# First layer's output projection in blocks of seven products, with ten low parts of weights by a negated copy and a transfer

## The chip, the cores and the metric

The kernel runs on one core of a Trainium2 chip. The metric is device time in microseconds (us) from start to end of one launch. The kernel before took 1089.74 us, the median of three runs (1089.67 to 1090.6). The core has five engines that run side by side, each through its own queue and in order: TensorE (PE in the profile) multiplies matrices and writes only to PSUM, VectorE (DVE) and ScalarE (ACT) do elementwise work, GpSimd (POOL) mostly issues transfers here, and SyncE (SP) issues the loads. An engine waits for another through a semaphore.

## The reference

Two transformer layers on 512 tokens of width 1024, in float32. Only the first layer's mixing matters here:

```python
proj = a @ w_in_a[layer]
u, v, q_mem = proj[..., :768], proj[..., 768:1536], proj[..., 1536:]
main = chunked_spatial_gating(u, v, w_s, b_s, ln_g, ln_b)     # 768 features: six groups of 128
mixed = concatenate([main, memory_attention(q_mem, mem_n, w_mem_kv[layer])], axis=-1)
h = h + rmsnorm(mixed @ w_out[layer], ln_mix_post[layer])     # the output projection: 1024 x 1024
```

After it comes a feed-forward (gate, up, down, with 2816 hidden features), then a second layer with causal attention in place of the gating.

## The kernel before, in words

**Precision.** TensorE is used in a reduced float32 type, so each operand `x` is kept as two parts: `hi`, a cast by ScalarE, and `lo = x - hi`, a subtraction by VectorE. The helper `split` makes both (L239), and `mm3` (L191 to L193) makes one product of three matmuls: hi by hi, hi by lo and lo by hi. Nearly all of the program's arithmetic runs through these two helpers, so the lines L191, L192, L193 and L239 stand for many places, and the tiles' names tell which: `whi`/`wlo` are parts of weights, `mixedhi`/`mixedlo` of the projection's inputs.

**The projection.** `mixed` is held as eight feature tiles of 128 features by 512 tokens. Tiles 6 and 7 are the memory attention's, 0 to 5 the spatial gating's, and `ORDER` puts 6, 7, 0, 1 first. One output tile `y` is 128 tokens (one of four token blocks, `tb`) by 512 of the 1024 output features (one of two halves, `dh`). In each matmul a 128 x 128 part of a feature tile is the stationary operand and 512 columns of weights are the moving one. `out_part` makes the first half of the sum, over the feature tiles 6, 7, 0, 1: two halves, four token blocks, four feature tiles and three matmuls each, 96 in all. Each finished tile is copied from PSUM to the tile `ys[tb][dh]` (L915). `mix_tail` and `tail_of` later add the feature tiles 2 to 5 (L846) and go on with the norm.

**Where it stands.** At the end of `layer_a` the gate blocks 1 to 5 (`gate_inputs`, 24 matmuls each) are put between the spatial blocks 0 to 5 (`spatial`, eight short matmuls each, then a chain over ScalarE and VectorE to the tile `sgu`, L765 to L770, which `store` splits into a feature tile of `mixed`). The first three spatial blocks lie between gate blocks, the last three between pieces of `out_part`: five, five and six pieces of six matmuls. The memory attention lies ahead of all this; its two feature tiles are put together from pairs of heads by `join` (L423, L424).

**Buffers.** Weights are loaded by SP's queue into four buffers `raw` of 128 x 1024, and their parts lie in eight buffers for `hi` and eight for `lo`, each 128 x 512. Three of these sixteen hold the spatial weights, one for every two spatial blocks: two among the `hi`, one among the `lo`. The activations' parts share 36 buffers, the float tiles `prob` six. PSUM has eight banks under three names: `tr` (2), `mm` (3) and `lg` (3). A buffer is given again when its last reader is done.

**What sets the order.** The program is written once, and a planner of the language lays out each engine's queue from it: at each step an engine gets, of what the planner expects to be ready, what was written first. Blocks under `high_priority` go ahead, and blocks under `issue_after` go behind a named instruction. On the chip the queues are then fixed, so an instruction whose input is late holds up all that stands behind it on its engine. SP's and GpSimd's transfers stand in such queues too.

**A pattern that is there already.** The feed-forward's down projection (`DownSeven`, `down_sevens`) makes 2 x 2 blocks with seven products instead of eight, and its class `Inner` makes some low parts through `split_aside`: ScalarE casts, ScalarE writes the negated high part (L1155), and a GpSimd transfer adds the source onto it in memory (L1156), so that VectorE is not needed. Copies from one PSUM tile to another are at L1270.

Of the kernel before, what the change touches and what calls it, by code (L numbers as in the profile page):

```python
# [7 lines left out]
F32 = mybir.dt.float32  # L8
# [32 lines left out]
def hybrid(ctx: ExitStack, tc: tile.TileContext, i: dict, out: bass.AP):  # L41
# [104 lines left out]

    def prepared(src, shape, aside=False):
# [16 lines left out]
    def moving_pair(src, aside=False):  # L164

        raw = wp.tile([P, 1024], F32, tag="raw", name=name("raw"), bufs=4)
        last_load[0] = nc.sync.dma_start(raw.rearrange("p (m c) -> p m c", m=4), src)
        four = raw.rearrange("p (m k c) -> p m k c", m=4, k=2)
# [69 lines left out]
    def split(src, hi, lo, eng=None):  # L238
        last_parts[:] = A.copy(hi, src), (eng or V).tensor_sub(lo, src, hi)  # L239

# [170 lines left out]

    joined = {}

    def join(o, mixed, m, j):


        own, _ = rows(j)
        if j == 0:
            mixed[m] = act("mixedhi"), act("mixedlo")
# [4 lines left out]
        V.tensor_add(joined[m][own, :], o[:64, :], f[:64, :])  # L424
        if j:
            return lambda: split(joined[m], *mixed[m])
# [163 lines left out]
    def layer_a():  # L590
# [55 lines left out]
        with tc.tile_pool(name="sgu", bufs=1) as lp:  # L646
# [60 lines left out]
            mixed = [None] * KT  # L707
            attend(mem_heads(0, q, mixed), between={n: take(fill, c) for n, c in enumerate((4, 4, 4, 4))})
# [46 lines left out]
            def spatial(g):  # L755
# [15 lines left out]
                store(t2, mixed, g)  # L771
# [124 lines left out]
    def out_part(layer, mixed):  # L896
# [22 lines left out]
        return ys, [block(dh) for dh in range(2)]  # L919

# [195 lines left out]
    def feed_forward(layer, phase, xp, meanwhile=None):  # L1116
# [33 lines left out]

        def split_aside(src, hi, lo, aside):
            if not aside:
                return split(src, hi, lo)
            A.copy(hi, src)
            A.activation(lo, hi, AF.Copy, scale=-1.0)  # L1155
            G.dma_start(lo, src, accum_op=ALU.add)  # L1156
# [485 lines left out]
```

## Time and profile before

| | |
|---|---|
| median of three runs | 1089.74 us |
| the profiled execution's own time | 1089.34 us |
| its span, first to last instruction | 1087.6 us |
| TensorE busy | 1079.2 us, 99% |
| VectorE busy | 971.8 us, 89% |
| ScalarE busy | 755.9 us, 69% |
| GpSimd busy | 93.5 us, 9% |
| granted TensorE clock, mean | 0.999 |

All times inside the profile are counted from the span's first instruction. A row of the instruction list gives the start, the duration, the engine, the line of the kernel, the operation, and `output<-inputs`; a bracket at its end tells how long the engine sat idle before it and who released it. A row of groups gives the count behind an x, then busy time and mean duration in ns. Matmuls overlap in the pipeline and their ends are modelled, so a matmul's pace is the distance between two starts, not its duration. Instructions of VectorE and ScalarE overlap by some 0.1 us in the same way. Rows of transfers give the time from issue to landing.

### The profile page before, as it was taken

The page shows a single profiled execution, that of the slowest core. Times are in us where ns is not written, and L with a number is a line of the kernel's source. Part 1 is how long each engine was busy: PE and PEld are TensorE (multiplying, and loading weights), DVE is VectorE, ACT ScalarE, POOL GpSimd, SP SyncE. Part 2 cuts the span into 40 slices and gives each one's busy share as a digit, 9 for nine tenths or more (in the row PEclk, how much of TensorE's full clock was granted, in tenths as well). Part 3 has the DMA queues.
Part 4 walks back from the last instruction along what each step waited for, and adds up shares of the span by engine and source line. Part 5 has one row for each costly group of instructions (what it writes and reads, how often), then busy time and mean ns, then how long its engine had stood idle before and what let it go on. Part 6 is the DMA issues. An engine that isn't in the chain of part 4 may idle for free.

```text
span 1087.6 us, 19810 instructions
## 1 busy us (share of the span) xinstructions
PE 1079.2 (99%) x7266; PEld 982.4 (90%) x7267; DVE 971.8 (89%) x1942; ACT 755.9 (69%) x1588; POOL 93.5 (9%) x120
## 2 busy tenths in 40 slices
PE   9999999999999999999999999999999999999998
PEld 8998889998989898998988998889997989898996
DVE  7879768999999999997968789868999999999986
ACT  7776578667766667577747788868666666757664
POOL 1000000002020202001000000000002010201100
PEclk9999999999999999999999999999999999999999
DMA  7421441338464664746222654531347465564632
GB/s 272 161 83 42 121 130 39 117 97 194 128 156 129 144 182 97 195 145 187 78 78 61 156 135 125 151 117 40 99 116 173 119 154 158 120 193 94 177 97 78
DMA packets 83993, 139.65 MB, mean 128 GB/s; under 512 B 6772, under 2 KB 49800, under 8 KB 83896
## 3 DMA queue, kind: packets, MB, share of 16 engines
q1 hardware_dynamic: 71480, 116.57, 34.9%
q0 software_dynamic: 11712, 21.50, 11.6%
q8 instruction: 57, 0.93, 0.4%
q10 hardware_dynamic: 704, 0.32, 0.1%
q14 instruction: 40, 0.33, 0.1%
HBM read 105.23 MB, written 2.10 MB: 99 GB/s over the span
## 4 chain that ended last, share of the span: by engine, by line
PE 71%; DVE 19%; DMA 4%; issue 3%; ACT 3%; SPq 0%; DVEq 0%; ACTq 0%
DVE wlo L239 6%; PE y L191 5%; PE y L192 5%; PE y L193 5%; PE ps L191 4%; PE ps L193 4%; PE ps L192 4%; DMA raw<-in_w_gate 4%; PE a L191 3%; PE a L192 3%; PE a L193 2%; PE v L191 2%; PE yc L191 2%; PE v L192 2%; PE v L193 2%
## 5 line engine op out<-in xcount | busy, mean ns | idle before, releaser
L239 ACT CAST whi<-raw 128x512 fp32r<-128x512 f32 x444 | 264.0, 620 | 100.7 <-DVE raw L1045 27.4
L239 DVE TENSOR_TENSOR wlo<-raw,whi 128x512 fp32r<-128x512 f32 x444 | 292.5, 687 | 22.1 <-ACT whi L239 21.2
L191 PE MATMUL x<-xshi,whi 128*128 128x256 f32 x320 | 90.0, 281 | 0.0
L193 PE MATMUL x<-xshi,wlo 128*128 128x256 f32 x320 | 90.0, 281 | 0.0
L191 PE MATMUL a<-xshi,whi 128*128 128x256 f32 x320 | 90.0, 281 | 0.0
L192 PE MATMUL x<-xslo,whi 128*128 128x256 f32 x320 | 89.9, 281 | 0.0
L192 PE MATMUL a<-xslo,whi 128*128 128x256 f32 x320 | 89.8, 281 | 0.0
L193 PE MATMUL a<-xshi,wlo 128*128 128x256 f32 x320 | 89.8, 281 | 0.0
L191 PE MATMUL ps<-xshi,whi 128*128 128x256 f32 (+1 forms) x224 | 68.5, 306 | 0.0
L192 PE MATMUL ps<-xslo,whi 128*128 128x256 f32 (+1 forms) x224 | 66.7, 298 | 0.0
L193 PE MATMUL ps<-xshi,wlo 128*128 128x256 f32 (+1 forms) x224 | 66.4, 298 | 0.0
L239 ACT CAST whi<-s 128x512 fp32r<-128x512 f32 x56 | 34.8, 621 | 38.8 <-DVE s L1208 18.6
L192 PEld LDWEIGHTS a<-xslo,whi 128*128 128x128 f32 x320 | 60.3, 189 | 0.4
L191 PEld LDWEIGHTS a<-xshi,whi 128*128 128x128 f32 x320 | 60.3, 188 | 0.4
L193 PEld LDWEIGHTS x<-xshi,wlo 128*128 128x128 f32 x320 | 60.4, 189 | 0.0
L192 PEld LDWEIGHTS x<-xslo,whi 128*128 128x128 f32 x320 | 60.3, 189 | 0.0
L193 PEld LDWEIGHTS a<-xshi,wlo 128*128 128x128 f32 x320 | 60.3, 189 | 0.0
L191 PEld LDWEIGHTS x<-xshi,whi 128*128 128x128 f32 x320 | 60.3, 188 | 0.0
L1243 POOL DMA_DIRECT2D y<-yo x48 | 41.4, 953 | 192.2 <-ACT yo L1242 130.8
L191 PE MATMUL y<-whi,mixedhi 128*128 128x512 f32 x128 | 51.4, 401 | 0.0
L192 PE MATMUL y<-wlo,mixedhi 128*128 128x512 f32 x128 | 50.7, 396 | 0.0
L193 PE MATMUL y<-whi,mixedlo 128*128 128x512 f32 x128 | 50.4, 394 | 0.0
(353 smaller groups left out, 3656.3 us busy)
## 6 DMA issues: line engine op xcount, KB each, us to landing
raw<-in_w_gate SPq DMA_DIRECT2D x44, 512.0 KB, 4.5
raw<-in_w_up SPq DMA_DIRECT2D x44, 512.0 KB, 5.7
y<-yo POOLq DMA_DIRECT2D x64, 256.0 KB, 4.9
raw<-in_w_down SPq DMA_DIRECT2D x28, 512.0 KB, 4.1
raw<-in_w_out SPq DMA_DIRECT2D x16, 512.0 KB, 4.0
wd<-in_w_down SPq DMA_DIRECT2D x32, 256.0 KB
flo<-s POOLq DMA_DIRECT2D x16, 256.0 KB, 4.8
raw<-in_w_b_q SPq DMA_DIRECT2D x8, 512.0 KB, 4.4
```

The source lines that it names most:

```text
L191: PE.matmul(o, w[0], x[0], start=start, stop=False, skip_group_check=more)
L192: PE.matmul(o, w[0], x[1], start=False, stop=False, skip_group_check=more)
L193: return PE.matmul(o, w[1], x[0], start=False, stop=stop, skip_group_check=more)
L239: last_parts[:] = A.copy(hi, src), (eng or V).tensor_sub(lo, src, hi)
L1243: G.dma_start(ys[to[0]][to[1]], some, accum_op=ALU.add)
```

## The change

The feature tiles 6 and 7 are one pair, 0 and 1 another. Each pair makes, with the two halves of the tokens and the two halves of the output features, a 2 x 2 by 2 x 2 block product, which now takes seven products of 128 features by 256 tokens by 512 output features, in place of eight.

- `PairInputs` collects a pair's two float tiles, forms four differences of half tiles in place (VectorE), and splits three and a half tiles into parts. `join` and `spatial` hand their tiles to it.
- `OutSeven` loads a pair's weights into two `raw` buffers, and a third tile `r3` on its own. Two GpSimd transfers from memory add weights onto `r3` and onto a quarter of the loaded tiles (`r1`). The remaining two sums of weights are VectorE additions.
- `weights(n)` prepares the parts for product `n`. For five of the seven products the low part goes by `split_aside`, in two pairs: ten low parts. The other four (products 7 and 1) are VectorE's subtractions.
- `out_sevens` makes the products of both pairs in the order 7, 1, 2, 6, 4, 5, 3, into four PSUM tiles that are held for the whole time: `chain` (both of `tr`) and `other` (two of `mm`). Between steps ScalarE copies `chain` onto `other`, and results leave by ScalarE's copies or VectorE's subtractions.
- Two steps follow the spatial block 3, two follow block 4, three follow block 5. The loads are written between the gate blocks, earlier than before.

The core of the diff:

```diff
+        def combine(self):
+            u0, u1 = self.us
+            left, right = (slice(*c) for c in HALVES)
+            first = act("b11", shape=(P, 2, 256))
+            second, both, other = [(act("mixedhi"), act("mixedlo")) for _ in range(3)]
+            split(u0[:, left], first[:, 0, :], first[:, 1, :])
+            split(u1, *second)
+            V.tensor_sub(u0[:, left], u0[:, left], u0[:, right])
+            V.tensor_sub(u0[:, right], u1[:, right], u0[:, right])
...
+            split(u0, *both)
+            split(u1, *other)
...
+    def split_aside(src, hi, lo, aside):
+        if not aside:
+            return split(src, hi, lo)
+        A.copy(hi, src)
+        A.activation(lo, hi, AF.Copy, scale=-1.0)
+        G.dma_start(lo, src, accum_op=ALU.add)
...
-            ys, outs = out_part(0, mixed)
-            more = queue(outs)
+            us_out = []
             for m in range(3, NG):
                 spatial(m - 3)
                 gate_inputs(m)
+                if m > 3:
+                    us_out.append(OutSeven(0, m - 4, pairs[m - 4]))
+            steps = list(out_sevens(us_out))
             for g in range(3, NG):
                 spatial(g)
-                for f in take(more, 5 if g < NG - 1 else 6):
+                for f in take(steps, 2 if g < NG - 1 else 3):
                     f()
+            [ys] = steps
...
+            self.a11, self.a12, self.r1, self.a22 = [r[:, :, x, :] for r in raws for x in range(2)]
+            self.r3 = prob("r3").rearrange("p (m c) -> p m c", m=4)
+            last_load[0] = nc.sync.dma_start(self.r3, src(0, 0))
+            G.dma_start(self.r3, src(1, 0), accum_op=ALU.add)
+            G.dma_start(self.r1, src(1, 1), accum_op=ALU.add)
+
+        def weights(self, n):
+            if n == 6:
+                V.tensor_add(self.a11, self.r1, self.a11)
+            if n == 3:
+                V.tensor_add(self.a12, self.a11, self.a12)
+            pair = pair_of_parts()
+            split_aside({1: self.a11, 2: self.a12, 3: self.a12, 4: self.a22, 5: self.r1, 6: self.a11, 7: self.r3}[n],
+                        *(t.rearrange("p (m c) -> p m c", m=4) for t in pair), n in (2, 6, 4, 5, 3))
+            return pair
...
+        def both(outs, n, done, start=False):
+            ws = [u.weights(n) for u in us]
+            for x, o in enumerate(outs):
+                for u, w in zip(us, ws):
+                    u.product(o, x, n, w, start and u is us[0], u is us[-1])
+                if done:
+                    done(x)
+
+        def leave(x):
+            A.copy(ys[x][0], other[x])
+
+        yield lambda: both(other, 7, lambda x: A.activation(some[x], other[x], AF.Copy, scale=-1.0), True)
+        yield lambda: both(chain, 1, lambda x: A.copy(other[x], chain[x]), True)
+        yield lambda: both(other, 2, leave)
+        yield lambda: both(chain, 6, lambda x: A.copy(other[x], chain[x]))
+        yield lambda: both(other, 4, lambda x: V.tensor_sub(ys[x][1], some[x], other[x]))
+        yield lambda: both(chain, 5, lambda x: V.tensor_sub(ys[x + 2][1], some[x], chain[x]))
+        yield lambda: both(chain, 3, lambda x: A.copy(ys[x + 2][0], chain[x]))
+        yield ys
```

More of the change, by code (lines that the diff above doesn't have):

```diff
@@ L164, in moving_pair @@
     def moving_pair(src, aside=False):
-        raw = wp.tile([P, 1024], F32, tag="raw", name=name("raw"), bufs=4)
-        last_load[0] = nc.sync.dma_start(raw.rearrange("p (m c) -> p m c", m=4), src)
-        four = raw.rearrange("p (m k c) -> p m k c", m=4, k=2)
+        four = loaded_four(src)
         parts = []
@@ L410, in store, with __init__, give @@
         split(src, *mixed[m])
+    class PairInputs:
+        def __init__(self):
+            self.us = []
+        def give(self, u):
+            self.us.append(u)
+            if len(self.us) == 2:
+                return self.combine
+        def combine(self):
[7 more added lines that the diff above has]
+            V.tensor_sub(u0[:, right], u1[:, right], u0[:, right])
+            V.scalar_tensor_tensor(out=u1[:, right], in0=u0[:, left], scalar=-1.0, in1=u1[:, right],
+                                   op0=ALU.mult, op1=ALU.subtract)
+            V.scalar_tensor_tensor(out=u1[:, left], in0=u1[:, right], scalar=-1.0, in1=u1[:, left],
+                                   op0=ALU.mult, op1=ALU.subtract)
+            split(u0, *both)
+            split(u1, *other)
+            half = lambda pair, c: tuple(t[:, c] for t in pair)
+            self.x = {1: (first[:, 0, :], first[:, 1, :]), 2: half(second, left), 3: half(second, right),
+                      4: half(other, left), 5: half(both, left), 6: half(other, right), 7: half(both, right)}
     joined = {}
@@ L417, in join @@
         own, _ = rows(j)
+        paired = isinstance(mixed[m], PairInputs)
         if j == 0:
-            mixed[m] = act("mixedhi"), act("mixedlo")
+            if not paired:
+                mixed[m] = act("mixedhi"), act("mixedlo")
             f = joined[m] = temp("f", tag="acc", bufs=2)
@@ L424, in join @@
         V.tensor_add(joined[m][own, :], o[:64, :], f[:64, :])
+        if j and paired:
+            return mixed[m].give(joined[m])
         if j:
@@ L919, in out_part, with __init__, product @@
         return ys, [block(dh) for dh in range(2)]
+    class OutSeven:
+        def __init__(self, layer, kp, inputs):
+            self.inputs = inputs
+            src = lambda dh, x: (i["w_out"][layer, 4 * dh : 4 * dh + 4, :, 256 * kp + P * x : 256 * kp + P * x + P]
+                                 .rearrange("m p c -> p m c"))
+            raws = []
+            for dh in range(2):
+                raw = loaded_four(i["w_out"][layer, 4 * dh : 4 * dh + 4, :, 256 * kp : 256 * kp + 256]
+                                  .rearrange("m p c -> p m c"))
+                raws.append(raw)
+            self.a11, self.a12, self.r1, self.a22 = [r[:, :, x, :] for r in raws for x in range(2)]
[12 more added lines that the diff above has]
+            return pair
+        def product(self, o, x, n, w, start, stop):
+            c = slice(x * P, (x + 1) * P)
+            return mm3(o, tuple(t[:, c] for t in self.inputs.x[n]), w, start, stop, True)
@@ new lines, in out_sevens @@
+    def out_sevens(us):
+        ys = [[plain("y") for _ in range(2)] for _ in range(TB)]
+        chain, other = [ps("tr", s="oc") for _ in range(2)], [ps("mm", s="ol") for _ in range(2)]
+        some = [prob("p7") for _ in range(2)]
+        def both(outs, n, done, start=False):
[15 more added lines that the diff above has]
+        yield ys
@@ L1149, in up_rows @@
                 split(u, *fs[len(fs) - 2 + row])
[L1151 to L1156, printed above, removed]
         class Inner:
```

12 lines of the change are left out of this document (11 added, 1 removed).

## The prediction

> **What bounds the kernel now.** I read the page's sums first, then a table of busy time by stage around the first layer's output projection, then TensorE's rows there in order of time.
>
> ```profile
> span 1087.6 us, 19810 instructions
> PE 1079.2 (99%) x7266; PEld 982.4 (90%) x7267; DVE 971.8 (89%) x1942; ACT 755.9 (69%) x1588; POOL 93.5 (9%) x120
> ```
>
> ```profile
> core 0: us, PE busy (x) PEld busy (x) DVE busy (x) ACT busy (x) POOL busy (x), PEclk, DMA share, GB/s
> 81.90:96.90 15.00, 14.94 (x76) 12.02 (x75) 14.01 (x38) 10.64 (x21) 1.31 (x1) 1.00 0.12 35
> 96.90:116.40 19.50, 19.50 (x98) 16.32 (x98) 19.28 (x40) 11.23 (x22) 0.00 (x0) 1.00 0.36 109
> 116.40:140.80 24.40, 24.40 (x115) 20.14 (x115) 17.04 (x29) 15.22 (x30) 0.00 (x0) 1.00 0.35 102
> ```
>
> The third stage is the projection's first half. TensorE has no idle time in it, so the stage is as long as its matmuls. VectorE is full in the stage before it (19.28 of 19.50) and has a quarter free in it (17.04 of 24.40); ScalarE is 62% busy (15.22). GpSimd does nothing.
>
> ```profile
> 116.45 0.45 PE L191 MATMUL y<-whi,mixedhi 128*128 128x512 f32 x1
> ...
> 123.47 0.28 PE L762 MATMUL s<-ws,vhi 128*128 128x256 f32 x1
> ...
> 124.33 0.45 PE L191 MATMUL y<-whi,mixedhi 128*128 128x512 f32 x1
> ...
> 131.38 0.28 PE L762 MATMUL s<-ws,vhi 128*128 128x256 f32 x1
> ...
> 132.23 0.45 PE L191 MATMUL y<-whi,mixedhi 128*128 128x512 f32 x1
> ...
> 140.64 0.39 PE L191 MATMUL y<-whi,mixedhi 128*128 128x512 f32 x1
> ```
>
> The first row opens the projection's 96 matmuls, the last is the first one after them (the tail). Between lie 24.19 us, less two spatial blocks of 0.86 and 0.85: 22.48 us, or 0.234 us a matmul.
>
> **The sum, part by part.** *Products.* 7 products x 2 pairs x 2 token blocks x 3 matmuls are 84 where there were 96, of the same 128x512 form. 12 x 0.234 = 2.81 us saved, if TensorE stays full. Nothing else in the change takes TensorE time away, so this is the whole gain; all that follows are losses against it.
>
> *Low parts of weights.* Per product after the first, both pairs need a high part, a low part that ScalarE writes negated, and a GpSimd transfer that adds the weight onto it. The rows are those of the same trick in the feed-forward (the lows of its inputs):
>
> ```profile
> L1155 ACT ACTIVATE flo<-fhi x16: 624/628/631, 230.1 to 985.8; 128x512 fp32r<-128x512 f32 x16
> L1156 POOL DMA_DIRECT2D flo<-s x16: 841/855/1047, 231.1 to 986.8; - x16
> ...
> DMA to landing us min/median/max: 3.3/4.8/7.2
> ```
>
> ```profile
> 127.79 1.14 ACT L239 CAST whi<-raw 128x512 fp32r<-128x512 f32 x2
> 139.19 2.50 DVE L239 TENSOR_TENSOR wlo<-raw,whi 128x512 fp32r<-128x512 f32 x4 [0.29 <-ACT whi L239]
> ```
>
> From the cast pair, one 128x512 costs ScalarE 0.52 us in a row (1.14 - 0.62); VectorE's subtraction costs 0.60 ((2.50 - 0.69) / 3). One low by the new way takes: cast 0.52, negated copy 0.63, 0.37 until the transfer is issued (231.1 - 230.1 - 0.63), 4.8 to landing: 6.3 us, where VectorE's took 0.52 + 0.69 = 1.2.
>
> How early can it start? The high parts rotate through 8 buffers; one holds spatial weights until the last spatial block, so 7 are free: three and a half steps of two. A step is 12 x 0.234 = 2.81 us. Laid out from 116.45 in the order 7, 1, 2, 6, 4, 5, 3, with spatial blocks after the second and fourth step, steps begin at 116.4, 119.2, 122.9, 125.7, 129.4, 132.2, 135.0 and end at 137.8. The second pair of the fourth, sixth and seventh steps takes over a buffer freed at 118.5, 125.0 and 127.8, and its low part is read 0.9 us into its step, at 126.7, 133.1 and 135.9: 8.1 us each time. That buffers, and no engine, set the start of such casts already shows today:
>
> ```profile
> 91.58 0.62 ACT L239 CAST whi<-raw 128x512 fp32r<-128x512 f32 x1 [1.15 <-PE ps L192]
> ```
>
> So 6.3 us must fit in 8.1, with 1.8 left for ScalarE's queue. Its work in the shortened stage (21.4 us without a stall):
>
> ```profile
> L239 ACT CAST whi<-raw 128x512 fp32r<-128x512 f32 x13 | 7.5, 620 | 0.2 <-PE y L193 0.2
> L915 ACT COPY y<-y 128x512 f32<-128x512 f32 x7 | 4.1, 584 | 5.3 <-PE y L193 5.2
> L765 ACT ACTIVATE s<-s,vcols 128x256 f32<-128x256 f32 x6 | 2.7, 471 | 1.2 <-PE s L763 1.2
> L239 ACT CAST mixedhi<-sgu 128x512 fp32r<-128x512 f32 x3 | 1.9, 620 | 2.0 <-DVE sgu L770 2.0
> L732 ACT ACTIVATE u<-u 128x512 f32<-128x512 f32 x1 | 0.6, 633 | 0.5 <-DVE u L731 0.5
> ```
>
> In 0.1 us less apiece when they follow each other, these are 6.8 + 3.4 + 2.3 + 1.6 + 0.5 = 14.6 us. Some nine casts and negated copies (four steps and half of the third) add 9 x 1.15 = 10.3, two more copies out of PSUM 1.0; two casts of the old projection go (1.0), and seven of the 13 that are for later stages can slip (3.6). That leaves 21.3 us in 21.4: ScalarE is full where it was at 62%. An in-order queue that full holds a cast back by one or two copies, 1 to 2 us. Landing at the median then just fits. From below, at 3.3 us, nothing is late. From above, at 7.2, each is 2.1 late (6.3 + 2.4 + 1.5 - 8.1); a stall also postpones the next release, so only two of the three add up: 4.2 us. I take 1.2, since 4.8 is the nearest row and the stage's queues are fuller than that row's. Queued behind a late cast on ScalarE are the copies out of PSUM, and TensorE's next step waits for those; behind its transfer on GpSimd only the next transfers.
>
> *Copies between PSUM tiles.* The third and the fifth step accumulate on what ScalarE copied from the other tile.
>
> ```profile
> L1270 ACT COPY ys<-yc x16: 564/583/605, 252.8 to 1007.0; 128x512 f32<-128x512 f32 x16
> ```
>
> 0.58 us each, under the other token block's six matmuls (1.4 us) and a spatial block (0.86): nothing. Without that cover 0.58 per copy, four copies.
>
> *Inputs.* Each pair needs 3.5 splits instead of 2 and four half-width differences:
>
> ```profile
> 248.78 0.42 DVE L1177 TENSOR_TENSOR s<-s,s 128x256 f32<-128x256 f32 x1
> 249.11 0.68 DVE L239 TENSOR_TENSOR wlo<-wd,whi 128x512 fp32r<-128x512 f32 x1
> ```
>
> 0.33 us per half width. VectorE: 1.5 x 0.60 + 4 x 0.33 = 2.2 us more per pair. The first pair falls among the layer norm's statistics after the attention (14.01 of 15.00 busy), where TensorE has gate blocks to go on with: nothing, or 2.2 if they cannot be brought forward. The second follows the second spatial block:
>
> ```profile
> 109.32 0.70 DVE L770 TENSOR_TENSOR sgu<-s,u 128x512 f32<-128x512 f32 x1
> ```
>
> From 110.0 its chain to the operand of product 7 is a cast and split of a half, two differences, a cast and a split: about 0.8 + 0.7 + 1.2 = 2.7 us alone, to be ready by 116.45. VectorE's sum before 116.45: + 4.4 for both pairs, + 2.4 for four low parts it keeps (products 7 and 1), + 1.2 for two weight sums, - 4.2 for seven low parts that it made there: 3.8 more in a queue without gaps. Between 0 (what is not urgent slips) and 3.8; I take 0.3, as 6.4 us lie between 110.0 and 116.45 for a chain of 2.7.
>
> *Loads.* The sums of weights take four GpSimd transfers out of memory onto loaded tiles, and two more loads on SP's queue. The raw weight buffers now stay in use until the last lows have landed, where they were free after two casts and subtractions, and the tail's loads wait for that on SP's queue:
>
> ```profile
> L167 SPq DMA_DIRECT2D raw<-in_w_out x3: 367/367/368, 107.3 to 111.2; - x3
> ...
> DMA to landing us min/median/max: 3.4/4.0/4.7
> ```
>
> The fourth weight load is the first of this row: 107.3 + 4.0 + 4.8 for the transfer onto it is 116.1, ahead of 118.5, when the fourth step's buffers come free: nothing, or what the landing exceeds 7.2 by. Last lows land about 137.1; + 4.0 is 141.1; + cast 0.62 and subtraction 0.69 is 142.4. TensorE asks for that half at 139.0 + 2.8 + 1.4 = 143.2. It fits by 0.8; the first loads are no better off. Between 0 and 2.1 (the wait in the next fence); I take 0.4. The feed-forward's loads move by some 8 us, with over 15 us to spare.
>
> ```profile
> 145.20 1.14 ACT L239 CAST whi<-raw 128x512 fp32r<-128x512 f32 x2 [2.13 <-DMA raw<-in_w_up]
> ```
>
> *Sum.* - 2.81 + 1.2 + 0.3 + 0.4 = - 0.9 us. The profiled execution took 1089.34 us (1087.6 of span and 1.74 around it), the median of the runs is 0.40 above: 1088.4 and 1088.8.
>
> **Rivals.** *All hidden.* The lows land in time and TensorE stays full: 1089.74 - 2.81 = 1086.9, up to 1087.5 with 0.6 lost. For it: 4.8 us is enough where ScalarE's queue is short. Against: a full ScalarE. The Trainium skill ("DMA: Bandwidth & Descriptors", section "Anatomy of one DMA — SWDGE (gpsimd) path") puts such a transfer at about 2.0 us plus its bytes over 436 GB/s, an estimate of 2.6 us for 256 KB, and by it this rival would hold; the rows above, at 3.3 to 7.2, do not agree.
>
> *The lows and the loads behind them are late: slower.* Such transfers issued right behind two others landed much later:
>
> ```profile
> L1266 POOL DMA_DIRECT2D y<-yo x16: 1507/1688/1879, 253.3 to 1007.5; - x16
> ...
> DMA to landing us min/median/max: 7.5/9.2/11.4
> ```
>
> At 7.2 us the steps lose 4.2; raw buffers then free late and ScalarE's queue stops at a cast whose load is not there, 2.1 by the row at 145.20. - 2.8 + 6.3 = + 3.5: 1093.2. It outweighs the gain once landing passes about 6.5 us. For it: lows come in twos beside loads. Against: 8 of the 16 lows in the nearest row landed in 4.8 or less. The Trainium skill ("SBUF — State Buffer", section "SBUF: two separate sides") warns that GpSimd cannot write descriptors while VectorE holds the port they share. The issue times here, 0.84 to 1.05 us beside a VectorE that is nearly full, do not show it.
>
> *The first product waits.* VectorE's 3.8 us come out ahead of product 7: some 3 us late there, after which the lows are early and lose little (0.2): + 0.4, 1090.1. For it: 19.28 of 19.50; against: it can let later spatial work slip.
>
> *Fewer products do not show.* TensorE's matmuls could run slower than 0.234 in the new order: about 1089.7. The feed-forward's products of this form speak against it.
>
> **How the numbers follow.** Forecast 0.43, all hidden 0.24, late lows 0.18, first product waits 0.12, no saving 0.03. About 0.2% (2.2 us) is what a measurement of this kernel can tell from no change: below 1087.6 lie nearly all of the first rival and a little of the forecast, 0.25; above 1091.9 lie most of the late lows and the ends of the others, 0.20; 0.55 between. The range, 1086.7 to 1092.6, leaves out about a tenth above. The forecast's own range is 1087.6 to 1090.3.
>
> **What will show it.** Right: 84 matmuls of 0.23 us; gaps of under 2 us on TensorE, released by a low part's transfer or ScalarE's copy; ScalarE over 90% busy in the stage; first product near 116.5. Wrong: a full TensorE (all hidden); lows landing at 7 us or a ScalarE waiting for a raw load (slower); a gap ahead of product 7 released by VectorE.

## The result, and the profile after

The changed kernel takes 1101.37 us (median of 5 runs, 1099.5 to 1103.65); the kernel before took 1090.09 us beside it. The ratio is 1.0102, 95% interval 1.009 to 1.0114: slower by 11.3 us where the forecast was 0.9 us faster, and far above the range's upper end of 1092.6. First the page's sums and the table by stage of the changed kernel, whose columns are those of the table before (busy time and instructions of each engine, granted clock, DMA share, GB/s).

```profile
span 1099.5 us, 19883 instructions
PE 1081.3 (98%) x7254; PEld 980.4 (89%) x7255; DVE 979.5 (89%) x1958; ACT 766.2 (70%) x1610; POOL 111.6 (10%) x134
```

```profile
96.90:116.40 19.50, 19.39 (x94) 16.10 (x95) 19.32 (x45) 12.20 (x24) 1.21 (x1) 1.00 0.29 69
116.40:140.80 24.40, 19.94 (x92) 14.76 (x90) 16.19 (x28) 18.66 (x37) 14.00 (x11) 1.00 0.87 99
140.80:163.00 22.20, 18.80 (x72) 14.60 (x73) 13.07 (x22) 13.16 (x27) 1.02 (x1) 0.92 0.96 268
```

The kernel before in the last of these stages, which the prediction's table does not show:

```profile
140.80:163.00 22.20, 22.20 (x104) 18.31 (x104) 12.28 (x24) 14.17 (x31) 1.65 (x3) 1.00 0.39 126
```

TensorE, full in both stages before, now stands 4.46 us of 24.40 and 3.40 us of the next 22.20. No other engine is full in its place: VectorE has 16.19 of 24.40, ScalarE 18.66. What is full is the column that the prediction did not price: the DMA engines' share went from 0.35 to 0.87, and in the next stage, where loads of weights that came later than before run too (268 GB/s), from 0.39 to 0.96. TensorE's rows of the changed kernel in order of time (start, duration, instruction, idle time ahead of it and what ended it):

```profile
117.64 0.45 PE L195 MATMUL ol<-whi,mixedhi 128*128 128x512 f32 x1
...
127.66 0.50 PE L196 MATMUL ol<-wlo,mixedhi 128*128 128x512 f32 x1 [1.29 <-DMA wlo<-raw]
...
131.18 0.50 PE L196 MATMUL oc<-wlo,mixedhi 128*128 128x512 f32 x1 [0.48 <-DMA wlo<-raw]
...
136.12 0.50 PE L196 MATMUL ol<-wlo,mixedhi 128*128 128x512 f32 x1 [0.98 <-DMA wlo<-raw]
...
141.10 0.50 PE L196 MATMUL oc<-wlo,mixedhi 128*128 128x512 f32 x1 [1.46 <-DMA wlo<-raw]
...
144.79 0.50 PE L196 MATMUL oc<-wlo,mixedhi 128*128 128x512 f32 x1 [1.57 <-DMA wlo<-raw]
...
147.28 0.50 PE L196 MATMUL oc<-wlo,mixedhi 128*128 128x512 f32 x1 [1.53 <-DMA wlo<-raw]
...
150.41 0.63 PE L197 MATMUL oc<-whi,mixedlo 128*128 128x512 f32 x1
150.84 0.59 PE L196 MATMUL y<-wlo,mixedhi 128*128 128x512 f32 x1
...
167.42 1.03 PE L943 MATMUL yt<-ident,y 128*128 128x128 f32 x8
```

The turns to the next layout in the kernel before (count, duration in ns, first and last start):

```profile
L888 PE MATMUL yt<-ident,y x112: 270/273/277, 157.2 to 1074.1; 128*128 128x128 f32 x112
```

Product 7 starts at 117.64, 1.2 us later than the projection did (116.45). From there to the tail's row at 150.84 are 33.2 us, where the prediction's layout had 21.4 (116.4 to 137.8). Every product from the third on waits for a low part's transfer, and behind the last gap the matmuls start 0.43 us apart instead of 0.23. The first turn to the next layout stands at 167.4 instead of 157.2 us: 10.2 us of the loss lie ahead of it. The other 1.7 us of the span come later in this execution; the runs below show at most 1.0 us there, and the rest stays unexplained. The transfers themselves, for the low parts in the changed kernel (min/median/max of the copy, of the issue in ns, and to landing in us), and the packets of their queue between 121 and 142 us (packets, MB, share of 16 engines):

```profile
L249 ACT ACTIVATE wlo<-whi x10: 617/626/638, 120.2 to 137.7; 128x512 fp32r<-128x512 f32 x10
L250 POOL DMA_DIRECT2D wlo<-raw x10: 1252/1264/1815, 121.1 to 138.8; - x10
...
DMA to landing us min/median/max: 4.2/5.0/8.4
```

```profile
q0 software_dynamic: 4224, 2.10, 89.9%
```

The landing, 5.0 at the median, is close to the 4.8 that the prediction took. But 4224 packets, nearly all of 512 B, took 89.9% of 16 engines for 21 us: 0.899 x 16 x 21 / 4224 = 71.5 ns of an engine each. A transfer of 256 KB is 512 packets (and 16 short ones), so it keeps all 16 engines for 512 x 71.5 / 16 = 2.3 us, and the two of a step for 4.6 us, where a step's matmuls last 2.81 us. In some rows below the DMA share is above 1.00, so packets' times can overlap on an engine, and these figures may be somewhat high. The waits fit them: those for the second pair's low part end at 127.66, 131.18, 136.12, 141.10 and 147.28 in products 2, 6, 4, 5 and 3, 4.9 us apart on average.

### The profile page after: what moved, and what is told of

Same layout as the page of the kernel before. It is cut to its first block, busy times and chain, and to the rows that moved or that the text cites. A ratio compares the mean times of both kernels' runs of the same rounds, so it can differ in the third digit from the quotient of the medians.

```text
span 1099.5 us, 19883 instructions
## 1 busy us (share of the span) xinstructions
PE 1081.3 (98%) x7254; PEld 980.4 (89%) x7255; DVE 979.5 (89%) x1958; ACT 766.2 (70%) x1610; POOL 111.6 (10%) x134
## 4 chain that ended last, share of the span: by engine, by line
PE 71%; DVE 16%; issue 4%; DMA 4%; ACT 3%; SPq 1%; POOL 0%; ACTq 0%; DVEq 0%; POOLq 0%
DVE wlo L243 5%; PE y L196 4%; PE y L195 4%; PE y L197 4%; PE a L195 3%; PE a L196 3%; PE a L197 3%; PE ps L195 3%; PE ps L196 3%; PE ps L197 3%; PE yc L195 2%; DMA raw<-in_w_gate 2%; PE x L197 2%; PE x L196 2%; PE x L195 2%
## 5 line engine op out<-in xcount | busy, mean ns | idle before, releaser
L243 ACT CAST whi<-raw 128x512 fp32r<-128x512 f32 x438 | 260.1, 620 | 101.3 <-DVE raw L1158 26.7
L243 DVE TENSOR_TENSOR wlo<-raw,whi 128x512 fp32r<-128x512 f32 x438 | 289.0, 688 | 25.5 <-ACT whi L243 24.3
L197 PE MATMUL x<-xshi,wlo 128*128 128x256 f32 x320 | 89.9, 281 | 0.0
L197 PE MATMUL e<-t3hi,wlo 128*128 128x256 f32 x160 | 45.1, 282 | 0.0
L196 PE MATMUL e<-t3lo,whi 128*128 128x256 f32 x160 | 45.0, 281 | 0.0
L197 PE MATMUL e<-t,wlo 128*128 128x256 f32 x160 | 45.0, 281 | 0.0
```

What stands on the lines that cost most here:

```text
L196: PE.matmul(o, w[0], x[1], start=False, stop=False, skip_group_check=more)
L197: return PE.matmul(o, w[1], x[0], start=False, stop=stop, skip_group_check=more)
```

## The experiments

Three theories stood against each other. By *rate*, the time that the transfers take of the DMA engines sets the steps. By *way*, the path of one low part (cast, copy, issue, landing) is too long for the buffers ahead, as the prediction weighed it. By *work*, what ScalarE and VectorE have to do besides makes the steps late. Ratios are against the kernel before on the same chip.

**All low parts by VectorE.** The ten go back to the plain split.

```diff
-                        *(t.rearrange("p (m c) -> p m c", m=4) for t in pair), n in (2, 6, 4, 5, 3))
+                        *(t.rearrange("p (m c) -> p m c", m=4) for t in pair), False)
```

> All fourteen low parts are VectorE's subtractions; the rest of the change stays. Theory A (the ten low parts are late by way of the negated copy and the transfer, and TensorE waits for them): the waits for transfers go, and 9 to 12 of the 11.3 us come back: 1088 to 1092, with TensorE gaps of under 2 us in the stage. Rival B (the blocks of seven themselves cost it: held PSUM tiles, copies between them, the pairs' combinations, raw buffers held longer): it stays within 3 us of the change, 1098 to 1102. Rival C (ScalarE is too full): its negated copies go here as well, so the same as A.

1093.3 us against 1090.19, ratio 1.0028 (1.0018 to 1.0038). The low parts' way by copy and transfer costs about 8 us, a little less than the 9 to 12 expected; without it the kernel is still 3.1 us slower. VectorE's busy time from 94.5 to 140 us, first in the kernel before, then in this one:

```profile
94.50:140.00 45.50, 45.50 (x229) 38.18 (x229) 37.92 (x73) 27.18 (x53) 0.00 (x0) 1.00 0.33 96
```

```profile
94.50:140.00 45.50, 43.88 (x217) 35.47 (x215) 43.43 (x88) 28.87 (x57) 3.16 (x3) 1.00 0.36 92
```

```profile
139.39 1.14 ACT L243 CAST whi<-raw 128x512 fp32r<-128x512 f32 x2 [2.86 <-DMA raw<-in_w_out]
...
141.08 0.69 DVE L243 TENSOR_TENSOR mixedlo<-sgu,mixedhi 128x512 fp32r<-128x512 f32 x1 [2.45 <-ACT mixedhi L243]
...
142.43 0.50 PE L195 MATMUL oc<-whi,mixedhi 128*128 128x512 f32 x1 [2.08 <-DVE y L1030]
```

The last fence holds ScalarE's, VectorE's and TensorE's rows of this run around 140 us. ScalarE stands for a tail load at a cast; VectorE then stands for ScalarE, with the copy of product 5 out of PSUM behind, and TensorE for that copy. This is the load's part of the prediction's slower rival, at its price of 2.1 us, although here no transfer of a low part holds the raw buffers.

**No transfer.** The low parts are left as the negated high parts; the work of adding the weights is left out.

```diff
-        G.dma_start(lo, src, accum_op=ALU.add)
+        if add:
+            G.dma_start(lo, src, accum_op=ALU.add)
```

> The ten transfers of the projection's low parts are left out and nothing replaces them, so those low parts are only the negated high parts and the result lacks the weights' share in them; ScalarE does all that it did. Theory A in its narrow form (the transfer's issue and landing, 5 to 8 us, is what is late): 8 to 11 us come back, 1090 to 1093. Rival C (ScalarE's order and load make the negated copies late, whatever follows): at most 4 come back, 1097 to 1101, and TensorE waits for ScalarE instead. Rival B: 1098 to 1102.

1091.0 us, ratio 1.0009 (0.9999 to 1.0018). ScalarE makes all its casts and copies here, and from product 7 to the first turn the run takes 38.8 us (121.22 to 160.0) instead of 40.7 (116.45 to 157.2): 1.9 of the 2.81 us are there. So ScalarE's added work is not the cause. Product 7 itself comes late in this execution, part of it under a lower granted clock ahead of it, and the transfers with what follows from them account for some 10 us (1101.4 less 1091.0). TensorE's row of product 7, and the rows of the turns:

```profile
121.22 0.45 PE L195 MATMUL ol<-whi,mixedhi 128*128 128x512 f32 x1
```

```profile
L944 PE MATMUL yt<-ident,y x112: 270/272/273, 160.0 to 1077.1; 128*128 128x128 f32 x112
```

**Whole rows.** Each 128x512 quarter of the weights is loaded as one contiguous block, so that a transfer reads 2 KB rows.

```diff
-                raw = loaded_four(i["w_out"][layer, 4 * dh : 4 * dh + 4, :, 256 * kp : 256 * kp + 256]
-                                  .rearrange("m p c -> p m c"))
-                raws.append(raw)
...
+                raws += loaded_apart(lambda x: src(dh, x))
...
```

> Each quarter of a pair's weights is loaded as one 128x512 tile whose row is contiguous, so that a transfer of a low part reads 2 KB at a time instead of four times 512 B; two loads of 256 KB stand for one of 512 KB. If the small packets make the transfers slow (issue 1.26 us where the feed-forward's take 0.86; 70 ns of a DMA engine for every 512 B): issue near 0.86 us, landing 1 us shorter, 3 to 6 us back: 1095 to 1098. If it is the path's length against the buffers: under 2 us back, 1099 to 1101.

1096.76 us, ratio 1.0058 (1.0045 to 1.0072): 4.6 us come back. **More buffers** put the pairs of products 6 and 4 into tiles of the activations' pool (`pair_of_parts(aside=n in (6, 4))`).

> The parts of the weights for products 6 and 4 lie in eight of the 36 activation buffers, so the eight and eight weight buffers serve five products and parts can be prepared two steps earlier. If the look-ahead of three and a half steps is what the 6 to 8 us of one low part's way do not fit into: 4 to 9 us back, 1092 to 1097. If DMA engines or ScalarE are the limit (their work is the same): under 3 us back, 1098 to 1101.

1102.19 us, ratio 1.0109 (1.0095 to 1.0122): nothing comes back.

**Plain transfers** keep number, rows and moment of the transfers but overwrite instead of adding (`plainly` is true for them alone), so the low parts hold the whole weights.

```diff
-        G.dma_start(lo, src, accum_op=ALU.add)
+        G.dma_start(lo, src, **({} if plainly else dict(accum_op=ALU.add)))
```

> Edit: the ten transfers of the changed kernel copy the raw weights over the negated high parts instead of adding to them, so the low parts hold the whole weights and the output is not the layer's; number, size, rows of 512 B and moment of the transfers stay. If the packets of 512 B set the rate (about 70 ns of an engine each, 2.2 us a transfer), nothing changes: 1100 to 1102, packets of 70 ns. If the adding sets it, the packets fall well below 70 ns, the landing from 4.2 us to 3.3 or less, and the time to 1094 to 1097.

1095.97 us, ratio 1.0054 (1.0038 to 1.0069). The queue's packets from 121 to 142 us, then issue (ns) and landing (us) of the ten, first in the run whole rows, then in the run plain transfers:

```profile
q0 software_dynamic: 1357, 2.48, 70.1%
```

```profile
L258 POOL DMA_DIRECT2D wlo<-raw x10: 828/847/1180, 121.5 to 137.5; - x10
...
DMA to landing us min/median/max: 3.3/3.6/6.3
```

```profile
q0 software_dynamic: 5274, 2.62, 72.2%
```

```profile
L250 POOL DMA_DIRECT2D wlo<-raw x10: 740/740/779, 121.6 to 137.3; - x10
...
DMA to landing us min/median/max: 2.7/2.9/5.7
```

By the same arithmetic a packet took 174 ns in whole rows, where a transfer is 144 of them (128 of 2 KB and 16 short ones): 1.6 us of all engines. Without the adding a 512 B packet took 46 ns, 1.5 us a transfer. Short rows and adding together make the 2.3 us, and taking away either is worth about 5 us. But either also shortens the issue (1.26 to 0.85 or 0.74 us) and the landing (5.0 to 3.6 or 2.9 us), so these two runs shorten the way along with the rate and do not part the two theories. Whole rows shows that the rate is not all: two transfers take 3.2 us of the engines a step there, yet the waits for the second pair's low parts of products 6, 4, 5 and 3 end at 130.09, 134.45, 138.99 and 143.86, 4.6 us apart. The Trainium skill ("DMA: Bandwidth & Descriptors", section "Why small descriptors are slow (HBM only)") holds that transfers inside SBUF do not suffer from short descriptors; for transfers that add, the changed kernel with 2.3 us and whole rows with 1.6 us differ from it.

**Half of the transfers.** Only the second pair's low parts are transferred, one per step.

```diff
+            self.inputs, self.second = inputs, kp == 1
...
-                        ..., n in (2, 6, 4, 5, 3))
+                        ..., self.second and n in (2, 6, 4, 5, 3))
```

> Edit: of the ten low parts five stay with the transfers (the second pair's, one of each of products 2, 6, 4, 5 and 3), five go back to VectorE. Theory of throughput (each 256 KB accumulating transfer in 512 B packets keeps the 16 DMA engines for about 2.2 us, so two per step take 4.5 us of DMA against 2.81 us of matmuls): one per step needs 2.2 us, fits, and the gaps in front of products 2 to 3 that end at a transfer go; the stage is then that of VectorE's own load, about 1092 (between 1091 and 1094). Theory of latency (a low part is late because cast, copy, issue and landing follow each other, 4.2 us for the landing whatever stands beside it): each step still holds one product pair that waits for its transfer, the landing stays near 4.2 us and the time near 1097 to 1100.

1095.56 us, ratio 1.0053 (1.0039 to 1.0067): between the two theories. Rows and adding are as in the changed kernel and only the number is halved, so one transfer's 2.3 us fits into a step: 5.8 of the 8.1 us come back, and the rest is not the rate. TensorE still stands for single transfers, issued about as late as before, and behind the longest gap its matmuls start 0.43 us apart. TensorE's rows of this run, and GpSimd's of its first transfer:

```profile
132.17 0.79 PE L196 MATMUL oc<-wlo,mixedhi 128*128 128x512 f32 x1 [2.34 <-DMA wlo<-raw]
132.76 0.63 PE L197 MATMUL oc<-whi,mixedlo 128*128 128x512 f32 x1
133.19 0.63 PE L195 MATMUL oc<-whi,mixedhi 128*128 128x512 f32 x1
```

```profile
122.56 1.26 POOL L250 DMA_DIRECT2D wlo<-raw  x1 [3.76 <-ACT wlo L249]
```

**Half ahead** gave these five pairs tiles of the activations' pool; **half lows apart** gave the five low parts tiles of the product copies' pool.

```diff
+            pair = pair_of_parts(aside=self.second and n in (2, 6, 4, 5, 3))      # half ahead
...
+            if self.second and n in (2, 6, 4, 5, 3):
+                pair = pair[0], tp.tile([P, T], F32R, tag="p", name=name("wlo"), bufs=6)      # half lows apart
```

> Edit: the run with half of the transfers (1095.6), and the high and low parts of its five go into tiles of the activations' pool, so that a cast, its copy and its transfer need not wait for a pair of parts of an earlier step. If a step's transfers fit the DMA engines (one of about 2.2 us per step of 2.81) and only their way of copy, issue and 4.2 us to the landing is too late, looking ahead takes the gaps of 2.3 and 1.5 us in front of products 6 and 5, and the lower clock behind the first of them: 1090.5 to 1092.5. If ScalarE, which stands at copies out of PSUM while TensorE waits, is what makes the next copy late, the buffers bring nothing: 1094.5 to 1096.5. With all ten transfers the same buffers brought nothing (1102.2 against 1101.4), which throughput alone explains.

> Edit: the run with half of the transfers (1095.6), and the low parts that are transferred lie in the pool of the product copies (six tiles, of which four are taken) instead of the ring of eight low parts that all products and gate blocks share. In the run half ahead the tiles of the activations' pool were free only from 131 us on, so nothing was ahead there. If the transferred low parts are late because their copy waits for a low part of the ring, the copy for product 2 moves from 121.6 us to some 117 to 119, the gaps before products 6 and 5 (2.3 and 1.5 us) shrink and the time is 1091.5 to 1093.5. If ScalarE's order (copies out of PSUM and the second pair's high parts ahead of it) makes them late, 1095 to 1096.

Half ahead took 1100.17 us, ratio 1.0096 (1.0082 to 1.011), and half lows apart 1095.45 us, ratio 1.005 (1.0036 to 1.0063). Half ahead missed both expectations. GpSimd's row of that run (the first below) shows where: its first transfer is issued at 133.22 instead of 122.56. The cast ahead of it stands at 130.97 in ScalarE's queue without a wait of its own, so the planner had put it that late; that it expected the activations' tiles to be free only then is likely, but no row shows it. Such tiles were no look-ahead here, so the run with more buffers proves less than its expectation says. In half lows apart (ScalarE's rows) the copy for product 2 still comes at 122.02:

```profile
133.22 1.26 POOL L250 DMA_DIRECT2D wlo<-raw  x1 [15.22 <-DVE wlo L243]
```

```profile
115.37 0.60 ACT L248 CAST whi<-raw 128x512 fp32r<-128x512 f32 x1
118.62 0.62 ACT L243 CAST mixedhi<-sgu 128x512 fp32r<-128x512 f32 x1 [2.65 <-DVE sgu L818]
...
122.02 0.62 ACT L249 ACTIVATE wlo<-whi 128x512 fp32r<-128x512 f32 x1
```

Its cast was done at 116, then ScalarE stood 2.65 us for VectorE's tile `sgu`, and the copy was in line behind what followed. So with five transfers it is ScalarE's order, and VectorE behind it, that makes them late: the way of a low part, but in a queue and not for want of low-part buffers. The changed kernel has the same wait of 2.65 us, at 118.12, and its first copies at 120.22.

**What is left without transfers.** *Tail apart* loads the tail's first block into tiles of the activations' pool; *first pair late* calls the first pair's combination after the fifth gate block; *products first* forms product 7's operand first in it; *combined early* gives it the planner's priority. All build on all low parts by VectorE.

```diff
+            return (act_weights if layer == 0 and dh == 0 else out_weights)(layer, 2 + kp, dh, aside)      # tail apart
-            return mixed[m].give(joined[m])      # first pair late
+            mixed[m].give(joined[m])
+            return None
...
+                    if m == 4:
+                        pairs[0].combine()
...
+                    if m == 4:
+                        with tc.high_priority():      # combined early
+                            pairs[0].combine()
```

> Edit: all ten low parts by VectorE as in the run all by VectorE (1093.3), and the four loads of the tail's first column block go into tiles of the activations' pool instead of the four raw buffers, so they need not wait until a raw buffer of a pair is read for the last time. If the tail stops because its weights' loads wait for the pairs' raw buffers (in the run all by VectorE ScalarE stood 2.86 us at a cast for its load, then VectorE 2.45 us for ScalarE, then TensorE 2.08 and 0.79 us), those gaps go: 1090.4 to 1091.3. If they come of VectorE being full to the end of product 3, nothing changes: 1093.0 to 1093.6.

> Edit: all ten low parts by VectorE as in the run all by VectorE (1093.3), and the first pair's combination (six vector operations and three casts that the last head group's join handed on) is called after the fifth gate block instead of among the attention's last joins. If the 1.2 us that TensorE loses at spatial block 0 come of VectorE doing this combination ahead of the value norm's parts, they return: the distance from the transpose of the gate columns to the first product falls from 23.1 to 22.0 us and the time to 1092.1. If they are only moved, because the same 2.2 us then stand ahead of the first product's low parts, the first product is as late as before: 1093.3.

> Edit: the run with the first pair's combination late (1090.9), and in the combination the sum that product 7 reads is formed and split ahead of the second tile's own parts, which only products 2 and 3 read. In that run TensorE stood 1.46 us at product 7 for this sum's high part. If that gap is just the order of VectorE's instructions, it goes (some 1.2 us of vector work are moved behind it): 1089.3 to 1089.8, no slower than before. If VectorE is full from there on, what is moved is late elsewhere, at products 1 to 3: 1090.5 to 1091.

> Edit: the run with the first pair's combination late (1090.9), and VectorE takes the combination ahead of whatever else stands ready (low parts of products 7 and 1, the gate pair's own work), as the planner's high priority. If VectorE's order is what is left, the gap of 1.46 us in front of product 7 goes and nothing replaces it: 1089.5 to 1089.9. If VectorE is full (it was busy 45.5 of 45.5 us there), what is pushed back stops TensorE somewhere else by as much, at a spatial block or product 1: 1090.5 to 1091.5.

Tail apart took 1093.51 us, ratio 1.0029 (1.0017 to 1.0041); first pair late 1090.9, ratio 1.0015 (1.0006 to 1.0024); products first 1091.94, ratio 1.0019 (1.001 to 1.0028); combined early 1090.6, ratio 1.001 (1.0001 to 1.0019). Tail apart gained nothing over all low parts by VectorE, but is inconclusive on the tail: its loads were issued from 137.45 us on, no earlier, since they stood in SP's queue behind two loads for the next stage. In its profile the gap of 2.08 us is gone (0.53 us at a cast is left), and from product 7 to the first turn it took 41.3 us instead of 42.0; but that execution was 1.5 us later already ahead of the spatial blocks. Products first let the planner begin product 1 ahead of product 7, and TensorE stood 0.59 us in the one and 1.51 us at the other. The late combination gives back some 2 us (2.4 by the medians, 1.4 by the ratios, whose intervals overlap), but not in the way expected. In the changed kernel TensorE waits for VectorE at the first spatial block (its row comes first); in first pair late that gap is gone and another stands at product 7 (the second row). The third fence is first pair late's busy time from 94.5 to 140 us:

```profile
96.90 0.33 PE L811 MATMUL s<-ws,vlo 128*128 128x128 f32 x1 [0.51 <-DVE vlo L243]
```

```profile
118.31 0.50 PE L195 MATMUL ol<-whi,mixedhi 128*128 128x512 f32 x1 [1.46 <-ACT mixedhi L243]
```

```profile
94.50:140.00 45.50, 42.99 (x215) 35.20 (x214) 45.40 (x92) 31.23 (x61) 1.63 (x2) 1.00 0.28 70
```

VectorE is busy for 45.40 of 45.50 us; in the three forms that change its order, TensorE stands at another place.

**Sums by GpSimd** takes the four sums of raw weights from VectorE, on top of first pair late.

```diff
-                V.tensor_add(self.a11, self.r1, self.a11)
+                G.tensor_add(self.a11, self.r1, self.a11)
```

> Edit: the run with all low parts by VectorE and the first pair's combination late (1090.9), and the four sums of raw weights for products 6 and 3 go from VectorE to GpSimd, which has nothing else to do there. VectorE is full from 94 to 142 us; this takes 2.4 us from it. If full VectorE is what eats the saving: 1088.3 to 1089.5. If GpSimd is so slow at 128x512 (over 3 us each, no row of before has one), or so disturbs VectorE, that product 6 or 3 waits for its weights: 1091 to 1094.

1095.21 us, ratio 1.0047 (1.0034 to 1.006): 4.3 us worse. GpSimd's and VectorE's rows of this run:

```profile
115.88 1.56 POOL L999 TENSOR_TENSOR raw<-raw,raw 128x512 f32<-128x512 f32 x1 [1.44 <-ACT whi L243]
```

```profile
116.24 1.49 DVE L442 TENSOR_TENSOR f<-f 128x256 f32<-128x256 f32 x1
```

VectorE's difference of two halves, 0.42 us in the prediction's row, lasted 1.49 beside GpSimd's sum and ended behind it. The Trainium skill ("SBUF — State Buffer", section "Who interferes with whom") says that an instruction of VectorE with two inputs in SBUF and one of GpSimd that reads SBUF shut each other out; these rows agree. The edit gave VectorE's time back to waiting, and TensorE stood 2.50 us at product 7, where first pair late had 1.46.

**Mixed forms.** *All three* joins whole rows, half of the transfers, tail apart and first pair late. *Early two* adds, to products first, transfers for products 4 and 5 of both pairs, called four steps ahead into the activations' pool. *Two early* transfers only the second pair's products 4 and 5, from whole rows, into tiles of their own, called at products 7 and 1; *two ahead*, on combined early, calls them at products 1 and 2; *two ahead rows* adds whole rows to it.

```diff
+            ws = [u.kept.pop(n) if n in u.kept else u.weights(n) for u in us]
+            if n in (1, 2):
+                m = {1: 4, 2: 5}[n]
+                us[1].kept[m] = us[1].weights(m)
```

> Edit: whole rows of 2 KB for the transfers' source (as in the run whole rows), five low parts by transfer and five by VectorE, the tail's first loads in tiles of the activations' pool, and the first pair's combination after the fifth gate block. Theory of throughput plus held buffers plus the first pair's combination: all three causes are taken away, 84 matmuls of 0.234 us fewer 12 remain to be saved: 1087.5 to 1089. If latency is the cause, the five transfers left still cost some 0.5 us each: 1091 to 1093.

> Edit: the run just described (products first), and the four low parts of products 4 and 5 come by ScalarE's copy and a transfer again, whose casts are called five and three steps ahead of their use, into tiles of the activations' pool; they read raw weights on which no vector sum is waiting. VectorE loses four instructions of 0.6 us in the stretch in which it is full (to 142), so that the evacuations of products 4 and 5 and the tail's low parts come earlier. If full VectorE is what is left of the loss: 1087.5 to 1089. If four transfers near each other slow the loads of the tail or hold ScalarE: 1090 to 1092.

> Edit: the run with the first pair's combination late (1090.9), raw weights loaded in whole rows of 2 KB, and only the second pair's low parts of products 4 and 5 come by ScalarE's copy and a transfer, into tiles kept free for them (high parts in the gate block's pool, low parts in that of the product copies), with the casts called at products 7 and 1. Two transfers of some 1.4 us of DMA each, four steps ahead of their use, stop nothing, and VectorE loses two instructions of 0.6 us: 1089.5 to 1090.3 if full VectorE is what is left. If even transfers with time to spare cost something (ScalarE's order, loads behind them), 1091.5 to 1094.

> Edit: the run combined early (1090.6), and the second pair's low parts of products 4 and 5 come by ScalarE's copy and a transfer into tiles kept free for them, their casts called at products 1 and 2, three steps ahead, when their raw loads have long landed (in the run two early a cast called at product 7 stood 1.63 us for its load and TensorE 4.14 us behind it). Rows of 512 B as in the changed kernel. If a transfer with time, buffer and source is free, VectorE's 1.2 us show: 1089.3 to 1090.2. If the landing of 4.2 us or ScalarE's order still stops TensorE: 1091 to 1093.

> Edit: the run two ahead with raw weights loaded in whole rows, so that the two transfers move packets of 2 KB. With two transfers far apart neither the rate nor the landing (3.3 instead of 4.2 us) should count: equal to the run two ahead within 0.5 us. If it is faster by more, the landing still counts; if slower, the raw loads in two halves (each of 256 KB) come later.

All three took 1095.85 us, ratio 1.0056 (1.0042 to 1.007); early two 1096.13, ratio 1.0056 (1.0044 to 1.0069); two early 1094.57, ratio 1.0043 (1.0031 to 1.0056); two ahead 1093.42, ratio 1.0034 (1.0021 to 1.0047); two ahead rows 1094.06, ratio 1.0041 (1.0029 to 1.0052). All five lie above every range that was expected of them. All three had 1.27 us of gap at product 7 and 0.7 to 1.2 us at three transfers. It is the run that leaves the rate out: five transfers of whole rows took 30.7% of the engines from 120 to 145 us, 1.5 us each, and TensorE stood for them all the same. The queue's packets and TensorE's rows of all three:

```profile
q0 software_dynamic: 720, 1.31, 30.7%
```

```profile
132.21 0.50 PE L217 MATMUL oc<-wlo,mixedhi 128*128 128x512 f32 x1 [0.70 <-DMA wlo<-raw]
...
136.93 0.50 PE L217 MATMUL ol<-wlo,mixedhi 128*128 128x512 f32 x1 [1.21 <-DMA wlo<-raw]
...
143.64 0.50 PE L217 MATMUL oc<-wlo,mixedhi 128*128 128x512 f32 x1 [0.92 <-DMA wlo<-raw]
```

Early two fell to the activations' pool again (first transfer at 131.93 us). The last three lost 3.2 to 4.1 us at product 7. Rows of ScalarE, TensorE and GpSimd in two ahead, then its table by stage:

```profile
115.53 0.62 ACT L248 CAST whe<-raw 128x512 fp32r<-128x512 f32 x1 [1.89 <-DMA raw<-in_w_out]
...
119.88 0.50 PE L195 MATMUL ol<-whi,mixedhi 128*128 128x512 f32 x1 [3.21 <-ACT mixedhi L243]
...
126.19 2.56 POOL L250 DMA_DIRECT2D wlo<-raw  x2 [13.89 <-PE oc L197]
```

```profile
122.00:128.00 6.00, 6.00 (x26) 4.88 (x26) 5.26 (x10) 4.65 (x10) 1.81 (x2) 0.85 0.00 0
128.00:134.00 6.00, 6.00 (x30) 4.94 (x30) 6.00 (x12) 5.28 (x12) 0.76 (x1) 1.00 0.84 97
134.00:140.00 6.00, 6.00 (x32) 5.03 (x31) 6.00 (x12) 4.96 (x10) 0.00 (x0) 1.00 1.04 337
```

A tile of its own let the planner put the cast far ahead of the call, and ScalarE stood 1.89 us at it for the raw load, with the first pair's high parts behind it; product 7 waited 3.21 us. The two transfers stopped nothing: TensorE is busy throughout from 122 to 140 us, though behind the gap at a granted clock of 0.85 in the first six. So two transfers in time cost nothing here, and a cast without its source did. No version beat the kernel before.

## Why the prediction was wrong, point by point

*Products.* Right as far as it shows. Where the transfers are left out, 1.9 of the 2.81 us appear in the steps.

*Low parts of weights.* This is the step that failed: "So 6.3 us must fit in 8.1 ... I take 1.2". It priced one low part's way by a landing seen among transfers further apart, and bounded it at 4.2 us. The row it borrowed was not of the same form either: the feed-forward's two transfers from 231 to 239.5 us moved 288 packets, whole rows of 2 KB, where two of the changed kernel move 1056. Ten transfers were asked for at two per step, and how much DMA time each takes was never set against the step: 4.6 us against 2.81. Nor was product 2 in the sum, whose copies stood in ScalarE's queue until 120.22. Measured, this way of making low parts costs 8.1 us (1101.4 less 1093.3) against the 1.2 that were taken. Halving the transfers gives 5.8 of it back, which the rate explains; all three shows that ScalarE's queue costs time without the rate. How the 8.1 us divide between the two stays open. The single gaps were all under 2 us, as the prediction's sign of being right had it, but seven of them add up to 7.8 us. Once TensorE waits, ScalarE's copies out of PSUM wait with it and the next low part's cast behind them; "a stall also postpones the next release" was seen, but was counted as ending by itself.

*ScalarE full.* Wrong for the changed kernel: 18.66 of 24.40, because it waits. Where nothing is transferred it has 21.41 of 24.40, so the sum of its work was about right. Its order counted, not its sum.

*Copies between PSUM tiles.* Nearly right: one gap of 0.46 us at product 2 ends at such a copy.

*Inputs.* "Nothing, or 2.2" for the first pair, with 0.3 taken at product 7. Product 7 starts 1.2 us late, and what made it late is VectorE at the first spatial block. The sum of VectorE's added work was worked out, but only against the time before product 7; in the form with all low parts by VectorE hardly any idle time is left to slip into (VectorE 43.43 of 45.50 busy).

*Loads.* Priced at 0.4, with 2.1 as its upper end. In the changed kernel the stall (ScalarE 4.54 us at a raw load, the row at 143.38 below) lies beside the late low parts; with all low parts by VectorE it shows by itself, 2.08 us on TensorE.

```profile
143.38 1.14 ACT L243 CAST whi<-raw 128x512 fp32r<-128x512 f32 x2 [4.54 <-DMA raw<-in_w_out]
```

*Rivals.* "The lows and the loads behind them are late" was the right one in sign and in its chain, at a third of the price (3.5 us against 11.3). Its deciding point was wrong: it was to outweigh the gain above a landing of 6.5 us, and the median was 5.0. "All hidden" falls. So does the Trainium skill's 2.6 us behind it ("DMA: Bandwidth & Descriptors", section "Anatomy of one DMA — SWDGE (gpsimd) path") for transfers that add: the shortest landing of the ten was 4.2 us. The plain transfers, with 2.7 us and up, are near it. "The first product waits" shows in the changed kernel with 1.2 us, which VectorE costs at a spatial block and not at product 7; at product 7 it shows in the forms with a late combination.

What stays open: the 3.1 us that the form with all low parts by VectorE is slower. In its profiled execution, whose span is 3.8 us longer, 0.9 us lie ahead of the first spatial block, 1.2 between it and product 7, and 1.3 between product 7 and the first turn, the saving of 2.81 already taken off; the rest comes later. VectorE's full queue fits the gaps there, and changes of order only moved them, but no run took work from VectorE without bringing in another wait.

## What to carry to other kernels

Price a repeated transfer twice: its landing against the look-ahead, and its engine time (packets by ns a packet, over 16 engines) against the period at which it repeats. Where the second exceeds the period, as 4.6 us did 2.81, each repetition falls further behind, and a small landing does not help. The first is not enough either: take such a price from a row with the same rows and the same adding, and count the place in the queue. When work is moved off an engine, ask in which in-order queue its pieces then stand, and behind which instruction that may have to wait.

## What the hardware showed that was not expected

Adding raised a 512 B packet from 46 to 71.5 ns and the issue on GpSimd from 0.74 to 1.26 us; with 2 KB rows the adding transfer issued in 0.85 us. And behind some gaps on TensorE the granted clock fell for about 3 us. In the changed kernel's table by stage:

```profile
145.00:150.00 5.00, 3.47 (x11) 2.42 (x11) 1.69 (x4) 1.62 (x3) 0.00 (x0) 0.78 1.05 302
```

The seven matmuls that start from 147.85 to 150.41 took 0.43 us each instead of 0.23, another 1.4 us. The equally long gap ahead of 141.10 was not followed by this, nor the one of 2.08 us in all low parts by VectorE; in all three one of 1.27 us was, and in no transfer one of 0.51 us (granted clock 0.66 from 100 to 105 us). So the length of a gap alone does not tell the loss.
